# A two-layer diffusion backbone on one core: five raw weight buffers, gate rows kept in DRAM, and the conditioning steps placed anew

## The chip, the core and the metric

The kernel runs on one core of a Trainium2 chip. The metric is the device time of one execution in microseconds (us), lower is better. TensorE (PE in the rows, PEld for its weight loads), VectorE (DVE), ScalarE (ACT), GpSimd (POOL) and SyncE (SP) each work through their own instructions in order; transfers are issued from SP, ACT or POOL.

## The reference

256 latent tokens and 256 context tokens of width 1024 go through two layers. A layer is a half-step gated feed-forward block (1024 to 2 x 2816 to 1024), a token mixer, and a second such block; the mixer of layer 0 is a recurrent RG-LRU block, that of layer 1 a windowed attention. Every block is normed before and after, and modulated by rows that come from a conditioning vector, one for the latent tokens and one for the context tokens:

```python
def modulate(h, g_pre, shift, scale):
    return rms_norm(h, g_pre) * (1 + scale) + shift

def modulation(cond, w, b):                 # w: (1024, 9*1024) for each layer
    m = jax.nn.silu(cond) @ w + b
    return jnp.moveaxis(m.reshape(cond.shape[0], N_MOD, D_MODEL), 1, 0)[:, :, None, :]

def half_ffn_update(h, mod, k, g_pre, g_post, w_in, w_out):
    y = swiglu(modulate(h, g_pre, mod[3 * k], mod[3 * k + 1]), w_in, w_out)
    return h + FFN_RES_WEIGHT * mod[3 * k + 2] * rms_norm(y, g_post)
...
for i in range(DEPTH):                      # x: latent, xc: context
    mx = modulation(c, w_mod[i], b_mod[i]); mc = modulation(c_ctx[None], w_mod[i], b_mod[i])
    x  = half_ffn_update(x, mx, 0, ...);  xc = half_ffn_update(xc, mc, 0, ...)
    ...                                     # mixer, gated by mx[5] and mc[5]
    x  = half_ffn_update(x, mx, 2, ...)     # and xc, except in the last layer
```

Of each layer's nine modulation rows, numbers 2, 5 and 8 are gates (they multiply a block's normed output) and the other six are scales and shifts ahead of a block.

## The kernel before

**Weights.** All weights are fp32 in DRAM. `wslot` (L107) loads 512 KB into a raw buffer `raw` (a ring of three, L47) on SP's queue, casts it on ACT to `whi` (L104) and has DVE form the rest `wlo` (L105); then the raw buffer is free again. `whi` and `wlo` have eight buffers each. `unit` (L120) and `tok_unit` (L135) make each product out of three matmuls (hi x hi, hi x lo, lo x hi), which stand at L127 to L129 and L142 to L144.

**A feed-forward block** (`ffn`, L380) first takes four column blocks j of the inner width, for the 256 latent and then for the 256 context tokens (matmuls of 256 columns), then the other eighteen with all 512 tokens. After each, `glu` (L346) runs: ACT silu into `s2`, DVE product into `a2` (L351), ACT cast into `dh`, DVE rest into `dl`. The 22 blocks are split in three groups; after groups 0 and 1 the product with `w_out` is added up in `y` (eight steps of 21 matmuls), after group 2 `out_last` (L361) finishes tile by tile: `post` (L182) multiplies by the gate row and adds to the residual `x`, `pre` (L196) norms it, `tick` turns the tile (L177, with `diag`) into the `hh` and `hl` of the next block.

**Modulation in the background.** `mod_job` (L289) makes one modulation row and is a generator. `bg(n)`, called after each `glu` (n = 2) and after each step of the `w_out` product (n = 1), advances the current job by n steps. Eight steps load 512 KB of `w_mod` each into a raw buffer and have DVE add it into `m` (L301, once for each of the two conditionings). The ninth sums over the partitions on PE (L307) and then does one of two things. For a scale or shift row: ACT copies the row out of PSUM (L331), PE transposes it into columns (`cols_of`, L256), DVE copies them to `modT`. For a gate row: it is multiplied by a norm row that was loaded into half of a `tmp` buffer (L320), written to DRAM (`spill`, L323) and at once read back, spread over all partitions, into 2 x 512 KB (L327): `grow_m` for the mixers, two `g4` buffers for the feed-forward blocks. These transfers and that of `b_mod` (L296) are issued from ACT's queue. The last gate row (1, 8) is made in `last_ffn` (L882).

**Order.** Tile writes out each engine's order from a model of the times, so a low-priority instruction may stand earlier than its place in the program. Buffers of one tag are handed out in program order.

Of the kernel before, what the change touches and what calls it, by code (L numbers as in the profile page):

```python
# [15 lines left out]
P = 128  # L16
# [20 lines left out]
class Net:  # L37
    def __init__(self, ctx, tc):
# [8 lines left out]
        self.rawp = e(tc.tile_pool(name="rawp", bufs=3))  # L47
# [12 lines left out]
        gm = self.big.tile([P, 2, D], F32, name="grow_m")  # L60
        self.grow_m = [gm[:, 0], gm[:, 1]]
# [29 lines left out]
    def grow_f(self):  # L91
        return [self.g4().rearrange("p a b -> p (a b)") for _ in range(2)]
# [166 lines left out]
    def mods_start(self, w_mod):  # L259
# [15 lines left out]
        row = self.tmp()[:, :512]  # L275
# [13 lines left out]
    def mod_job(self, l, m, conds=(0, 1), grow=None, f=1.0):  # L289
# [3 lines left out]
        for c in conds:  # L293
            acc[c] = self.m4().rearrange("p a b -> p (a b)")
            v.memset(acc[c], 0.0)
            nc.scalar.dma_start(acc[c][0:1], self.b_mod[l : l + 1, m * D : (m + 1) * D])  # L296
# [17 lines left out]
        row = self.tmp()  # L314
        if grow is not None:
            row, gq = row[:, :512], row[:, 512:]
# [63 lines left out]
    def ffn(self, w_in, w_out, bg, after, mid=None):  # L380
# [5 lines left out]
        for s in (LAT, CTX):  # L386
            for j in range(NSPLIT):
# [4 lines left out]
                self.glu(ps[:, 0], ps[:, 1], j, s)  # L392
        for gi, (j0, j1) in enumerate(GROUPS):
# [27 lines left out]
def net_kernel(  # L421
# [117 lines left out]
    def mj(l, m, **kw):  # L539
        return lambda: N.mod_job(l, m, **kw)  # L540

    grow = N.grow_f()
    bg = bg_runner(
        [mj(0, 2, grow=grow, f=0.5), mj(0, 3), mj(0, 4), mj(0, 5, grow=N.grow_m), mj(0, 6), mj(0, 7)]
    )
    N.ffn(ffn_w_in[0, 0], ffn_w_out[0, 0], bg, boundary(grow, 0, 1), load_ctx)

    rg_mixer(N, rg_w_in[0], rg_gate_w[0], rg_w_out[0], rgT, boundary(N.grow_m, 0, 2))

    grow = N.grow_f()  # L550
    bg = bg_runner([mj(0, 8, grow=grow, f=0.5), mj(1, 0), mj(1, 1), mj(1, 3), mj(1, 4)])
    N.ffn(ffn_w_in[0, 1], ffn_w_out[0, 1], bg, boundary(grow, 1, 0))

    grow = N.grow_f()
    bg = bg_runner(
        [mj(1, 2, grow=grow, f=0.5), mj(1, 5, conds=(1,), grow=N.grow_m), mj(1, 6, conds=(1,)), mj(1, 7, conds=(1,))]
    )
    N.ffn(ffn_w_in[1, 0], ffn_w_out[1, 0], bg, boundary(grow, 1, 1))

    attn_mixer(  # L560
        N, attn_w_qkv[0], attn_w_o[0], attn_sink, k_perm, k_rope, k_mask, boundary(N.grow_m, 1, 2, (1,))
    )

    last_ffn(N, ffn_w_in[1, 1], ffn_w_out[1, 1], out)


def rg_mixer(N, w_in, gate_w, w_out, rgT, after):
# [125 lines left out]
    N.out_last(vo, 0, NK, False, TILES, dh, dl, after)  # L693


def attn_mixer(N, w_qkv, w_o, sink, k_perm, k_rope, k_mask, after):
# [89 lines left out]

    wv = [N.wslot([vq[:, 4 * b : 4 * b + 4, NQ + NKVD : NQ + 2 * NKVD]]) for b in range(2)]
# [94 lines left out]
def last_ffn(N, w_in, w_out, out):  # L882
# [3 lines left out]
    grow = N.grow_f()  # L886
    job = N.mod_job(1, 8, conds=(1,), grow=grow, f=0.5)
# [134 lines left out]
```

## Time and profile before

| | us |
|---|---|
| time, median of 3 runs | 1767.45 (1767.33 to 1769.81) |
| span of the profiled execution | 1767.6 |
| PE matmul busy | 1692.1 (96%) |
| DVE busy | 1148.4 (65%) |
| ACT busy | 718.5 (41%) |
| mean DMA rate | 143 GB/s |

The span of the profiled execution, from its first instruction to its last, is within 0.2 us of the median time, so sums over the span are sums over the time. Busy time of PE is what its matmuls occupy, at either of TensorE's clocks; idle time of the other engines costs nothing as long as PE does not wait for them.

### The profile page before, as it was taken

How to read it: one execution, taken by the hardware profiler on the slowest of the kernel's cores; microseconds unless marked ns; L12 is line 12 of the kernel's file. 1: busy time of each engine (PE TensorE's matmuls, PEld its weight loads, DVE VectorE, ACT ScalarE, POOL GpSimd, SP SyncE). 2: the span in 40 equal slices, each digit the busy share in tenths (PEclk: the TensorE clock that was granted, in tenths of full speed). 3: DMA queues.
4: the chain of work that ended last, by engine and by line, in shares of the span. 5: the costliest groups of instructions: out<-in, count | busy, mean ns of one | idle time of the engine just before them, and what ended most of it. 6: DMA issues, size and time to landing. Idle time of an engine off the chain costs nothing.

```text
span 1767.6 us, 22913 instructions
## 1 busy us (share of the span) xinstructions
PE 1692.1 (96%) x8980; PEld 1432.1 (81%) x8980; DVE 1148.4 (65%) x1798; ACT 718.5 (41%) x1148; POOL 0.2 (0%) x4
## 2 busy tenths in 40 slices
PE   5999899999999999989999999998999999999998
PEld 4988688878988798868787898876888888879897
DVE  4756667777878766556874666355333799765554
ACT  3432222235699453122133353132232577564442
POOL 0000000000000000000000000000000000000000
PEclk9999999999999999989999999999999999999999
DMA  8565456572322246445574156576432231057662
GB/s 295 158 177 173 137 155 201 170 222 85 101 75 72 72 139 180 142 132 172 173 210 124 35 145 180 157 225 207 115 96 84 75 104 61 14 153 230 215 207 71
DMA packets 262084, 253.56 MB, mean 143 GB/s; under 512 B 8780, under 2 KB 213028, under 8 KB 261976
## 3 DMA queue, kind: packets, MB, share of 16 engines
q1 hardware_dynamic: 256800, 244.35, 45.7%
q10 hardware_dynamic: 5176, 7.76, 1.5%
q8 instruction: 70, 1.15, 0.3%
q14 instruction: 38, 0.31, 0.1%
HBM read 250.97 MB, written 1.10 MB: 143 GB/s over the span
## 4 chain that ended last, share of the span: by engine, by line
PE 55%; DMA 14%; DVE 13%; ACT 7%; issue 3%; ACTq 0%; DVEq 0%
PE mm L129 11%; PE mm L127 11%; PE mm L128 11%; DMA raw<-in_ffn_w_in_dram 7%; PE mm L142 5%; PE mm L144 5%; PE mm L143 5%; DMA raw<-in_w_mod_dram 4%; DVE wlo L105 4%; DVE m L301 3%; ACT whi L104 3%; DMA raw<-in_ffn_w_out_dram 2%; PE st L838 1%; PE st L177 1%; ACT tmp L217 1%
## 5 line engine op out<-in xcount | busy, mean ns | idle before, releaser
L127 PE MATMUL mm<-hh,whi 128*128 128x512 f32 (+1 forms) x1808 | 617.1, 341 | 2.5 <-ACT hh L247 2.1
L129 PE MATMUL mm<-hh,wlo 128*128 128x512 f32 (+1 forms) x1808 | 616.4, 341 | 2.0 <-DVE wlo L105 2.0
L128 PE MATMUL mm<-hl,whi 128*128 128x512 f32 (+1 forms) x1808 | 615.9, 341 | 0.1
L104 ACT CAST whi<-raw 128x1024 fp32r<-128x1024 f32 x322 | 332.1, 1035 | 569.5 <-DMA raw<-in_ffn_w_in_dram 252.3
L105 DVE TENSOR_TENSOR wlo<-raw,whi 128x1024 fp32r<-128x1024 f32 x322 | 386.1, 1203 | 270.3 <-ACT whi L104 267.8
L127 PEld LDWEIGHTS mm<-hh,whi 128*128 128x128 f32 x1808 | 346.1, 192 | 47.5 <-issue 4.2
L129 PEld LDWEIGHTS mm<-hh,wlo 128*128 128x128 f32 x1808 | 346.2, 192 | 39.5 <-DVE wlo L105 2.6
L128 PEld LDWEIGHTS mm<-hl,whi 128*128 128x128 f32 x1808 | 345.8, 191 | 38.0 <-DVE hl L249 0.7
L301 DVE SCALAR_TENSOR_TENSOR m<-raw,cs,m 128x1024 f32<-128x1024 f32 x224 | 279.6, 1278 | 50.2 <-DMA raw<-in_w_mod_dram 49.2
L142 PE MATMUL mm<-whi,dh 128*128 128x512 f32 x592 | 232.8, 396 | 7.5 <-ACT dh L104 5.0
L143 PE MATMUL mm<-wlo,dh 128*128 128x512 f32 x592 | 232.5, 393 | 1.1 <-DVE wlo L105 0.9
L144 PE MATMUL mm<-whi,dl 128*128 128x512 f32 x592 | 231.9, 392 | 0.5 <-DVE dl L105 0.5
L142 PEld LDWEIGHTS mm<-whi,dh 128*128 128x128 f32 x592 | 112.1, 190 | 38.2 <-ACT dh L104 5.5
L143 PEld LDWEIGHTS mm<-wlo,dh 128*128 128x128 f32 x592 | 112.2, 189 | 26.0 <-DVE wlo L105 3.4
L144 PEld LDWEIGHTS mm<-whi,dl 128*128 128x128 f32 x592 | 112.0, 189 | 24.3 <-DVE dl L105 1.2
L351 DVE TENSOR_TENSOR a<-s,mm 128x512 f32<-128x512 f32 (+1 forms) x96 | 54.3, 566 | 77.9 <-PE mm L129 59.9
L104 ACT CAST dh<-a 128x512 fp32r<-128x512 f32 (+1 forms) x96 | 50.5, 527 | 132.1 <-DVE a L351 132.0
L350 ACT ACTIVATE s<-mm 128x512 f32<-128x512 f32 (+1 forms) x96 | 48.2, 502 | 72.8 <-PE mm L129 70.0
L105 DVE TENSOR_TENSOR dl<-a,dh 128x512 fp32r<-128x512 f32 (+1 forms) x96 | 54.5, 567 | 14.4 <-ACT dh L104 14.1
L177 PE MATMUL st<-diag,xres 128*128 128x128 f32 x352 | 47.8, 292 | 13.1 <-DVE diag L170 10.3
L177 PEld LDWEIGHTS st<-diag,xres 128*128 128x128 f32 x352 | 45.1, 204 | 17.8 <-DVE diag L170 10.1
L217 ACT ACTIVATE tmp<-st,modT,A 128x128 f32<-128x128 f32 x144 | 55.2, 470 | 6.4 <-PE st L177 6.3
(189 smaller groups left out, 1364.5 us busy)
## 6 DMA issues: line engine op xcount, KB each, us to landing
raw<-in_ffn_w_in_dram SPq DMA_DIRECT2D x176, 512.0 KB
raw<-in_w_mod_dram SPq DMA_DIRECT2D x128, 512.0 KB
raw<-in_ffn_w_out_dram SPq DMA_DIRECT2D x82, 512.0 KB
wm<-in_w_mod_dram SPq DMA_DIRECT2D x16, 512.0 KB
raw<-in_rg_w_in_dram SPq DMA_DIRECT2D x16, 512.0 KB
raw<-in_attn_w_qkv_dram SPq DMA_DIRECT2D x12, 512.0 KB
raw<-in_rg_gate_w_dram SPq DMA_DIRECT2D x16, 256.0 KB
raw<-in_rg_w_out_dram SPq DMA_DIRECT2D x8, 512.0 KB
```

Source lines behind the costliest of these rows:

```text
L104: self.nc.scalar.copy(hi, src)
L105: self.nc.vector.tensor_tensor(lo, src, hi.bitcast(F32), op=ALU.subtract)
L127: nc.tensor.matmul(out, a, xh, start=(k == 0), stop=False)
L128: nc.tensor.matmul(out, a, xl, start=False, stop=False)
L129: nc.tensor.matmul(out, b, xh, start=False, stop=(k == nk - 1))
L142: nc.tensor.matmul(out, a, wh, start=(k == 0), stop=False)
L143: nc.tensor.matmul(out, a, wl, start=False, stop=False)
L144: nc.tensor.matmul(out, b, wh, start=False, stop=(k == nk - 1))
L177: self.nc.tensor.matmul(ps[:, q * P : (q + 1) * P], self.x[:, t, k * P : (k + 1) * P], dg, start=True, stop=True)
L217: nc.scalar.activation(hf[:, k * P : (k + 1) * P], ps[:, q * P : (q + 1) * P], AF.Identity, bias=S[:, k, cond : cond + 1], scale=A[:, k, c ...
L301: v.scalar_tensor_tensor(acc[c], raw, self.cs[:, k, c : c + 1], acc[c], op0=ALU.mult, op1=ALU.add)
L351: nc.vector.tensor_tensor(b, a, pu, op=ALU.mult)
```

## The change

Five things are changed together.

1. The ring `raw` gets five buffers in place of three; `grow_m` (8 KB of each partition) is gone.
2. A gate row stays in DRAM (`spill`, kept in `rows`) after it is made. `load_rows` spreads it over the partitions where it is wanted: just ahead of `out_last` in a feed-forward block and in `rg_mixer` (into two `g4` buffers), after the keys in `attn_mixer` (into the context's residual tile 0, which the second layer's end does not need), and at the start of `last_ffn` (residual tile 1).
3. All these small transfers, and those of `b_mod` and the norm row, go to GpSimd's queue. The copied rows and norm rows stand in `s2` and `a2` instead of `tmp`.
4. For a scale or shift row there is a `yield` between ACT's copy and PE's transposes, so they are two steps (ten a job).
5. In the first part of each `ffn` there is one step more after each `glu` (in the very first block only for the context half), and the job of row (1, 8) moves from `last_ffn` to the block before the attention.

```diff
-        self.rawp = e(tc.tile_pool(name="rawp", bufs=3))
+        self.rawp = e(tc.tile_pool(name="rawp", bufs=5))
...
-        gm = self.big.tile([P, 2, D], F32, name="grow_m")
-        self.grow_m = [gm[:, 0], gm[:, 1]]
+        self.rows = {}
...
+    def grow_g4(self):
+        return {c: self.g4().rearrange("p a b -> p (a b)") for c in range(2)}
+
+    def load_rows(self, key, grow):
+        for c, dst in grow.items():
+            for hb in range(2):
+                j = 2 * hb + c
+                self.nc.gpsimd.dma_start(
+                    dst[:, hb * 512 : hb * 512 + 512], self.rows[key][j : j + 1].to_broadcast((P, 512))
+                )
+        return grow
...
-            nc.scalar.dma_start(acc[c][0:1], self.b_mod[l : l + 1, m * D : (m + 1) * D])
+            nc.gpsimd.dma_start(acc[c][0:1], self.b_mod[l : l + 1, m * D : (m + 1) * D])
...
+        if f is not None:
+            gq = self.s2()
...
-                nc.scalar.dma_start(gq[32 * j : 32 * j + 32], self.norm_g[l, gi : gi + 1, cc].to_broadcast((32, 512)))
+                nc.gpsimd.dma_start(gq[32 * j : 32 * j + 32], self.norm_g[l, gi : gi + 1, cc].to_broadcast((32, 512)))
+            row = self.a2()
             v.scalar_tensor_tensor(row, ps, f * RS, gq, op0=ALU.mult, op1=ALU.mult)
...
-            nc.scalar.dma_start(spill, row[0:P:32])
-            for c in conds:
-                for hb in range(2):
-                    j = 2 * hb + c
-                    nc.scalar.dma_start(grow[c][:, hb * 512 : hb * 512 + 512], spill[j : j + 1].to_broadcast((P, 512)))
+            nc.gpsimd.dma_start(spill, row[0:P:32])
+            self.rows[l, m] = spill
             yield
             return
-        row = row[:, :512]
+        row = self.s2()
         nc.scalar.copy(row, ps)
+        yield
         tv = self.cols_of(row)
...
                 self.glu(ps[:, 0], ps[:, 1], j, s)
+                if mid is None or s is CTX:
+                    bg(1)
...
                 bg(1000)
+                rows()
                 self.out_last(vo, j0, j1, True, TILES, self.dh, self.dl, after)
...
+    lat = dict(conds=(1,))
+    ffn(0, 0, [mj(0, 2, f=0.5), mj(0, 3), mj(0, 4), mj(0, 5, f=1.0), mj(0, 6), mj(0, 7)], 0, 1, load_ctx)
+    rg_mixer(N, rg_w_in[0], rg_gate_w[0], rg_w_out[0], rgT, lambda grow: boundary(grow, 0, 2))
+    ffn(0, 1, [mj(0, 8, f=0.5), mj(1, 0), mj(1, 1), mj(1, 3), mj(1, 4)], 1, 0)
+    ffn(
+        1,
+        0,
+        [mj(1, 2, f=0.5), mj(1, 5, f=1.0, **lat), mj(1, 6, **lat), mj(1, 7, **lat), mj(1, 8, f=0.5, **lat)],
+        1,
+        1,
     )
...
+        lambda: after_attn.update(N.load_rows((1, 5), {1: N.x[:, 0]})),
+        boundary(after_attn, 1, 2, (1,)),
     )
...
+    last_ffn(N, ffn_w_in[1, 1], ffn_w_out[1, 1], N.load_rows((1, 8), {1: N.x[:, 1]}), out)
...
+    grow = N.load_rows((0, 5), N.grow_g4())
+    N.out_last(vo, 0, NK, False, TILES, dh, dl, after(grow))
...
-    grow = N.grow_f()
-    job = N.mod_job(1, 8, conds=(1,), grow=grow, f=0.5)
...
-        if j >= 6:
-            next(job, None)
```

## Rows read from the trace of the kernel before

**Rows 1.** The page's first lines: span, and busy time and share of each engine.

```profile
span 1767.6 us, 22913 instructions
PE 1692.1 (96%) x8980; PEld 1432.1 (81%) x8980; DVE 1148.4 (65%) x1798; ACT 718.5 (41%) x1148; POOL 0.2 (0%) x4
```

**Rows 2.** What PE waited for, over the span: us in total, times, longest us.

```profile
PE st L256 <- ACT tmp L331: 16.8, 4, 6.6
PE st L177 <- DVE diag L170: 10.3, 8, 1.9
...
PE mm L142 <- ACT dh L104: 5.0, 1, 5.0
PE st L898 <- DVE dl L105: 3.1, 3, 1.8
...
PE mm L129 <- DVE wlo L105: 2.0, 2, 1.2
```

**Rows 3.** Stretches of the span: from:to, length, then busy us (and instructions) of PE, PEld, DVE, ACT and POOL, the granted TensorE clock (1.00 is full), the DMA engines' busy share, GB/s.

```profile
186.80:192.40 5.60, 0.00 (x0) 0.00 (x0) 2.80 (x4) 2.15 (x3) 0.00 (x0) 0.69 0.19 40
192.40:195.80 3.40, 3.35 (x10) 2.86 (x11) 2.51 (x5) 0.00 (x0) 0.00 (x0) 0.50 0.34 134
777.10:782.80 5.70, 5.56 (x15) 4.55 (x16) 4.78 (x8) 0.09 (x1) 0.00 (x0) 0.50 0.20 80
936.70:939.90 3.20, 3.20 (x10) 2.72 (x11) 2.52 (x6) 0.00 (x0) 0.00 (x0) 0.50 0.77 247
1230.80:1236.80 6.00, 5.40 (x12) 3.81 (x13) 2.94 (x6) 0.02 (x1) 0.00 (x0) 0.50 0.95 282
1639.60:1643.00 3.40, 3.40 (x12) 2.72 (x11) 1.38 (x2) 0.73 (x2) 0.00 (x0) 0.50 0.83 240
```

**Rows 4.** The instructions around the first of these stalls, in order of time on PE, ACT and SP: start, duration, and in brackets the idle time before and what ended it.

```profile
192.45 1.11 PE L256 MATMUL st<-ident,tmp 128*128 128x128 f32 x4 [5.68 <-ACT tmp L331]
...
188.36 1.04 ACT L104 CAST whi<-raw 128x1024 fp32r<-128x1024 f32 x1 [5.06 <-DMA raw<-in_ffn_w_in_dram]
191.82 0.58 ACT L331 COPY tmp<-st 128x512 f32<-128x512 f32 x1
...
184.09 0.38 SPq L113 DMA_DIRECT2D raw<-in_ffn_w_in_dram  x1
```

**Rows 5.** What SP's queue waited for before it could issue a load, over the span (L113 weights, L299 `w_mod`).

```profile
SPq L113 <- DVE wlo L105: 770.9, 201, 63.8
SPq L299 <- DVE m L301: 187.9, 50, 17.6
```

**Rows 6.** What ACT waited for, over the span.

```profile
ACT whi L104 <- DMA raw<-in_ffn_w_in_dram: 252.3, 105, 8.3
ACT whi L104 <- DMA raw<-in_ffn_w_out_dram: 133.8, 57, 16.2
```

**Rows 7.** Stretches as in rows 3: the first part of the second block, the start, a feed-forward block, the last block, and the end of the block before the attention.

```profile
617.00:640.00 23.00, 21.08 (x156) 19.91 (x155) 19.07 (x43) 18.68 (x40) 0.00 (x0) 1.00 0.64 181
20.00:40.00 20.00, 16.39 (x100) 9.03 (x99) 8.23 (x28) 7.46 (x12) 0.00 (x0) 0.88 0.97 331
740.00:760.00 20.00, 20.00 (x90) 16.56 (x89) 14.27 (x12) 5.66 (x8) 0.00 (x0) 1.00 0.80 232
1600.00:1700.00 100.00, 96.52 (x656) 88.08 (x655) 58.04 (x63) 41.10 (x54) 0.00 (x0) 0.98 0.72 221
1240.00:1360.00 120.00, 120.00 (x536) 98.47 (x535) 44.55 (x51) 34.46 (x41) 0.00 (x0) 1.00 0.35 102
```

**Rows 8.** DVE and PE at the end of a group in the block before the attention, in order of time.

```profile
1223.31 1.29 DVE L301 SCALAR_TENSOR_TENSOR m<-raw,cs,m 128x1024 f32<-128x1024 f32 x1 [2.95 <-DMA raw<-in_w_mod_dram]
...
1228.29 1.28 DVE L301 SCALAR_TENSOR_TENSOR m<-raw,cs,m 128x1024 f32<-128x1024 f32 x1 [2.56 <-DMA raw<-in_w_mod_dram]
1229.49 0.68 DVE L351 TENSOR_TENSOR a<-s,mm 128x512 f32<-128x512 f32 x1
...
1230.87 0.80 PE L142 MATMUL mm<-whi,dh 128*128 128x512 f32 x1 [5.03 <-ACT dh L104]
```

**Rows 9.** DVE in `last_ffn` around one of PE's waits for `dl`, in order of time.

```profile
1637.00 1.28 DVE L301 SCALAR_TENSOR_TENSOR m<-raw,cs,m 128x1024 f32<-128x1024 f32 x1 [1.37 <-DMA raw<-in_w_mod_dram]
1638.20 0.42 DVE L105 TENSOR_TENSOR dl<-a,dh 128x256 fp32r<-128x256 f32 x1
```

**Rows 10.** DVE and PE in the first part of the block before the attention, in order of time: the end of the last tile's norm (L170) and the turn that needs it (L177).

```profile
1032.27 1.28 DVE L301 SCALAR_TENSOR_TENSOR m<-raw,cs,m 128x1024 f32<-128x1024 f32 x1 [0.67 <-DMA raw<-in_w_mod_dram]
...
1034.28 1.28 DVE L301 SCALAR_TENSOR_TENSOR m<-raw,cs,m 128x1024 f32<-128x1024 f32 x1
1035.47 0.28 DVE L170 TENSOR_SCALAR diag<-ident,small 128x128 f32<-128x128 f32 x1
...
1035.81 1.38 PE L177 MATMUL st<-diag,xres 128*128 128x128 f32 x10 [1.89 <-DVE diag L170]
```

**Rows 11.** ACT's small transfers at the end of the first gate row's job, in order of time.

```profile
140.42 0.58 ACTq L323 DMA_DIRECT2D spill<-tmp  x1
143.67 1.80 ACTq L327 DMA_DIRECT2D g<-spill  x4
```

**Rows 12.** DVE at the end of `rg_mixer`: the last reading of a `g4` buffer and the first use of the gate row.

```profile
577.94 0.68 DVE L678 TENSOR_TENSOR y<-g,g 128x512 f32<-128x512 f32 x1
...
594.67 1.41 DVE L190 SCALAR_TENSOR_TENSOR tmp<-mm,small,grow_m 128x512 f32<-128x512 f32 x2
```

More of the change, by code (lines that the diff above doesn't have):

```diff
@@ L89, in a2 @@
         return self.ph.tile([P, T], dt, tag="a2", name=self.nm("a2"), bufs=2)
-    def grow_f(self):
-        return [self.g4().rearrange("p a b -> p (a b)") for _ in range(2)]
+    def grow_g4(self):
[8 more added lines that the diff above has]
+        return grow
     def c(self, shape, dt, name):
@@ L274, in mods_start @@
                     )
-        row = self.tmp()[:, :512]
+        row = self.s2()
         nc.scalar.copy(row, ps)
@@ L287, in mods_start, with mod_job @@
                     )
-    def mod_job(self, l, m, conds=(0, 1), grow=None, f=1.0):
+    def mod_job(self, l, m, conds=(0, 1), f=None):
         nc = self.nc
@@ L313, in mod_job @@
                 )
-        row = self.tmp()
-        if grow is not None:
-            row, gq = row[:, :512], row[:, 512:]
+        if f is not None:
+            gq = self.s2()
             gi = 3 + m // 3
@@ L319, in mod_job @@
                 cc = slice((j // 2) * 512, (j // 2) * 512 + 512)
-                nc.scalar.dma_start(gq[32 * j : 32 * j + 32], self.norm_g[l, gi : gi + 1, cc].to_broadcast((32, 512)))
+                nc.gpsimd.dma_start(gq[32 * j : 32 * j + 32], self.norm_g[l, gi : gi + 1, cc].to_broadcast((32, 512)))
+            row = self.a2()
             v.scalar_tensor_tensor(row, ps, f * RS, gq, op0=ALU.mult, op1=ALU.mult)
             spill = self.tc.dram_tile([4, 512], F32, name=self.nm("spill"))
-            nc.scalar.dma_start(spill, row[0:P:32])
-            for c in conds:
-                for hb in range(2):
-                    j = 2 * hb + c
-                    nc.scalar.dma_start(grow[c][:, hb * 512 : hb * 512 + 512], spill[j : j + 1].to_broadcast((P, 512)))
+            nc.gpsimd.dma_start(spill, row[0:P:32])
+            self.rows[l, m] = spill
             yield
             return
-        row = row[:, :512]
+        row = self.s2()
         nc.scalar.copy(row, ps)
+        yield
         tv = self.cols_of(row)
@@ L378, in out_last, with ffn @@
                 self.tick(2)
-    def ffn(self, w_in, w_out, bg, after, mid=None):
+    def ffn(self, w_in, w_out, bg, rows, after, mid=None):
         nc = self.nc
@@ L540, in mj, with ffn @@
         return lambda: N.mod_job(l, m, **kw)
-    grow = N.grow_f()
-    bg = bg_runner(
-        [mj(0, 2, grow=grow, f=0.5), mj(0, 3), mj(0, 4), mj(0, 5, grow=N.grow_m), mj(0, 6), mj(0, 7)]
-    )
[L546 to L556, printed above, removed]
-    )
[L558 to L564, printed above, removed]
+    def ffn(l, k, jobs, l2, k2, mid=None):
+        grow = {}
+        N.ffn(
+            ffn_w_in[l, k],
+            ffn_w_out[l, k],
+            bg_runner(jobs),
+            lambda: grow.update(N.load_rows((l, 2 + 6 * k), N.grow_g4())),
+            boundary(grow, l2, k2),
+            mid,
+        )
+    lat = dict(conds=(1,))
[8 more added lines that the diff above has]
+        1,
+    )
+    after_attn = {}
+    attn_mixer(
+        N,
+        attn_w_qkv[0],
+        attn_w_o[0],
+        attn_sink,
+        k_perm,
+        k_rope,
+        k_mask,
+        lambda: after_attn.update(N.load_rows((1, 5), {1: N.x[:, 0]})),
+        boundary(after_attn, 1, 2, (1,)),
+    )
+    last_ffn(N, ffn_w_in[1, 1], ffn_w_out[1, 1], N.load_rows((1, 8), {1: N.x[:, 1]}), out)
 def rg_mixer(N, w_in, gate_w, w_out, rgT, after):
@@ L691, in rg_mixer, with attn_mixer @@
         prev = ins
-    N.out_last(vo, 0, NK, False, TILES, dh, dl, after)
-def attn_mixer(N, w_qkv, w_o, sink, k_perm, k_rope, k_mask, after):
+    grow = N.load_rows((0, 5), N.grow_g4())
+    N.out_last(vo, 0, NK, False, TILES, dh, dl, after(grow))
+def attn_mixer(N, w_qkv, w_o, sink, k_perm, k_rope, k_mask, rows, after):
     nc = N.nc
@@ L785, in attn_mixer @@
                 )
+    rows()
     wv = [N.wslot([vq[:, 4 * b : 4 * b + 4, NQ + NKVD : NQ + 2 * NKVD]]) for b in range(2)]
@@ L879, in attn_mixer, with last_ffn @@
     proj(1, 1)
-def last_ffn(N, w_in, w_out, out):
+def last_ffn(N, w_in, w_out, grow, out):
     nc = N.nc
@@ L885, in last_ffn @@
     vo = w_out.rearrange("(j p) c -> p j c", p=P)
-    grow = N.grow_f()
-    job = N.mod_job(1, 8, conds=(1,), grow=grow, f=0.5)
     po = {}
```

## The prediction, made before the changed kernel was run

> **What bounds the kernel now.** I read the page first: PE is busy in 1692.1 of 1767.6 us, DVE in 65% and ACT in 41% [rows 1]. The matmuls themselves stay as they are, so no edit can gain more than PE's idle 75.5 us and the time it works at the half clock. The next view is what PE waited for [rows 2]: the largest wait, 16.8 us in four pieces, is that of the transposes (L256) for ACT's copy; then come 10.3 us for the norm's `diag`, 5.0 for one `dh`, 3.1 for `dl`, 2.0 for `wlo`. The third view, short stretches around these waits, shows the second price [rows 3]: PE sits idle from 186.8 to 192.4, and then runs at clock 0.50 (1.2 instead of 2.4 GHz) until 195.8. Each longer idle time is followed by such a stretch, and half of a stretch is lost.
>
> Why is a copy of 0.58 us late by 5.7? The instructions around it show it [rows 4]: ACT's queue is in order, and ahead of the copy stood a cast that waited 5.06 us for its weights. That load was issued at 184.09, only when one of the three raw buffers came free. SP's queue tells the same over the span: 770.9 us, 201 times, it waited for a raw buffer that `wlo` still held, and 187.9 us for one held by `m` [rows 5]. ACT in turn waited 252.3 and 133.8 us for loads [rows 6]. PE is mostly covered, since eight `whi` and `wlo` stand ahead of it; what reaches it is what is queued on ACT or DVE behind a late load: a copy, a `dh`, a `dl`, a `diag`.
>
> **The change part by part.**
>
> *Transposes a step later.* The four waits cost 16.8 us, and the half-clock stretches after three of them 3.40, 5.70 and 3.20 us, of which half is lost: 1.7 + 2.85 + 1.6 = 6.15. Together 22.95 us. I went through the calls of `bg` to see what stands between the two steps now. Seven of ten jobs get 21 to 48 matmuls between copy and transposes (at 20.00 / 90 = 0.222 us each [rows 7], 4.7 us or more): `dh`, copy and all are done by then. In three, both steps fall into one call, with nothing between: (0, 6) after block 17, (0, 7) at the end of the first feed-forward block, and (1, 6) after block 9. For those the old risk stays: 3 of 10 jobs at a mean of 22.95 / 3 = 7.65 us for each stall, and 3 of 10 stalled at length before, is 3 x 0.3 x 7.65 = 6.9 us; with a deeper ring I take half, 3.4 (bounds 0 and 22.95). Gain **19.6**.
>
> *Five raw buffers.* Is the ring or the DMA rate the limit? With sixteen loads in flight at the start the chip moved 331 GB/s at a DMA share of 0.97; in a feed-forward block with three it reached 232 at 0.80, and it needs some 196 there (four loads of 0.524 MB for each 48 matmuls of 0.222 us = 10.7 us) [rows 7]. So three buffers leave little above the need, and five leave up to 331. Where does a late load reach PE other than by the copies? At the end of a group [rows 8] DVE's product `a` stands behind two `m`, which waited 2.95 and 2.56 us for `w_mod`; PE waited 5.03 us for the `dh` made from it and then ran six us at the half clock, 3.0 lost: 8.0 us. I take four fifths, 6.4 (bounds 0 and 8.0; the same `m` can stand there with its load in place). Of the waits for `wlo`, 2.0 us [rows 2], I take 1.5. Gain **7.9**.
>
> *The job of row (1, 8).* It leaves the last block, which ran at 221 GB/s and kept PE idle for 3.5 of 100 us [rows 7], and whose `dl` stood behind an `m` that waited 1.37 us for its load [rows 9]. The waits for `dl`, 3.1 us, and half of the 3.40 at half clock go: **4.8**. In the block before the attention it costs eight `m` of 1.28 = 10.2 us of DVE, and there DVE is busy 44.6 of 120 us at 102 GB/s: nothing, while that room lasts. Its sums on PE (L307) are made in the one place as in the other.
>
> *Steps in the first part.* The first `w_mod` steps of the two later blocks are now due while the last tile is still normed and turned. What that does is seen in the block before the attention [rows 10]: two `m` got in between the norm's small operations, 1.28 us each and 0.67 of waiting, and PE waited 1.89 us for `diag`. In the block before that, none did. I charge two more `m` in each, 2 x 2 x 1.28 = 5.1 us: **-5.0**. Bounds: 0, if `diag` keeps its priority, and four steps of 2.56 us in each of the three first parts, 30.7.
>
> *Small transfers on GpSimd's queue, rows in DRAM.* ACT loses its issues (one spill 0.58, four row loads 1.80, [rows 11]); PE didn't wait for those, so I take 0. The bounds: a gain of nothing, since ACT is idle 59% of the span; a loss where a row comes late. `post` needs the row first about 11 us after `out_last` starts, and in the feed-forward blocks the buffers and the spilled rows are ready long before. In `rg_mixer` the `g4` buffers come free only at 577.94 + 0.68 = 578.6, and the row is used at 594.67 [rows 12]: 16 us. From a spill's issue to the row load that needs it it is 143.67 - 141.00 = 2.7 us [rows 11]; four loads of 256 KB at 232 GB/s take 4.5 more, 7.2 in all: covered. POOL did 0.2 us of work before [rows 1]; nothing else is queued there but the next blocks' `b_mod`, which came after that point before, too. The swap of `tmp` for `s2` and `a2` costs nothing while `glu`, every 10.7 us, holds its buffer for 1 to 2 us: one of two is always free.
>
> One rule speaks against this edit. The Trainium skill (SBUF — State Buffer, SBUF: two separate sides) says that a transfer issued from GpSimd needs descriptors which GpSimd cannot write while VectorE runs an operation that takes both of its ports, and gives 3.1 us in place of 0.62 for such a transfer. No run here shows such a transfer yet. By its figure four row loads take an estimated 12.4 us, still under the 16; its case is the last rival below.
>
> **Sum.** 19.6 + 7.9 + 4.8 - 5.0 = 27.3 us; 1767.6 - 27.3 = 1740.3, say **1740**. The span and the median of the runs, 1767.45, are the same for this purpose.
>
> **The rivals.**
> - *The rate, not the ring, is the limit.* Five loads share what three shared, each lands later, and ACT and DVE wait as long as before. For it: the share of 0.95 at 282 GB/s in one stretch [rows 3]. Against it: SP's waits [rows 5], and 232 against 331 [rows 7]. Then the ring gives none of its 7.9 and the three unparted jobs cost 6.9: 27.3 - 7.9 - 3.5 = 15.9, **1752**.
> - *The ring does more.* The loads land so early that `diag`, `dh` and the unparted copies meet no queue: the remaining 3.4 and 1.6 are gained, nothing is charged for the first parts, and half of the 10.3 for `diag` goes: 27.3 + 3.4 + 1.6 + 5.0 + 5.1 = 42.4, **1725**.
> - *The turn is not later.* The order is written from modelled times, and the transposes at 192.45 [rows 4] did not stand straight behind their sums; if the planner puts them back to the copy, 19.6 is lost: 7.7 remain, **1760**. Against it: their place in the program is now behind a block's matmuls, which are ready.
> - *Slower: DVE is overrun in the first parts.* In 617 to 640 DVE was busy 19.07 of 23 us [rows 7], and four steps more of 2.56 are 10.2: 29.3 in 23. If `hl` and `diag` stand behind them, PE waits 6.3 us in each of three first parts, and a wait of that length brought 1.6 to 3 us at the half clock: some 9 each, 27 in place of the 5 charged: 1767.6 - 27.3 + 22 = 1762. From 32.3 / 3 = 10.8 us each the kernel is slower; with loads waited for in between, 13 each gives **1774**. Against it: PE turns the last tile only 14 us into the block, and `pre` has priority.
> - *Slower: the row comes late in `rg_mixer`.* Beyond 16 us every us is one of PE's, and the half clock follows. It decides when the load ends 27 us late, 43 us for four loads: 11 each, four times what the 2.7 us [rows 11] bear out; at 13 each the time is 1767.6 - 27.3 + 36 = **1776**.
>
> **How the numbers follow.** Chances: the forecast (1733 to 1747) 0.42; the rate 0.20; the ring does more 0.16; the turn not later 0.06; gains and new waits cancel 0.05; DVE overrun 0.08, and the row late 0.03. Runs of one kernel lie 0.14% apart, so 0.2% (3.5 us) is what can be told from no change. Faster: 0.42 + 0.20 + 0.16 + 0.06 = 0.84, less 0.01 for the upper edge of the DVE case, which I count as slower; same 0.05; slower 0.12. The range runs from the far side of "the ring does more" (bounds of the same terms, 5 us further: 1720) to the third rival's 1760, and leaves out the 0.05 and 0.12, and some 0.03 at either edge.
>
> **What the new profile would show.** Right: no wait of L256 for the copy over 1 us except at the three unparted jobs; SP's waits for `wlo` and ACT's for loads well under 770.9 and 386; rates above 232 GB/s inside a block; no wait for `dl` in the last block. Wrong: a wait for `diag` above 1.9 us early in the second or third block, clock 0.50 in a first part, PE waiting for `post` after `rg_mixer`, or ACT's waits for loads as long as before.

## The result and the profile after

The changed kernel takes 1725.24 us (median; 1724.68 to 1725.57) where the kernel before took 1767.39 beside it: a ratio of 0.9766 [0.9752, 0.9780], 42.2 us faster. The forecast was 1740 with a range of 1720 to 1760. The direction and the range hold, the size doesn't: the gain is half as large again as the 27.3 us of the sum, and the time lands on the rival "the ring does more", 1725.

The head of the page after, the lines that answer to [rows 1]:

```profile
span 1723.8 us, 23005 instructions
PE 1678.0 (97%) x8980; PEld 1425.6 (83%) x8980; DVE 1139.6 (66%) x1798; ACT 716.5 (42%) x1148; POOL 40.3 (2%) x82
```

The span is 43.8 us shorter, and the two numbers of PE divide it. Its idle time goes from 75.5 to 1723.8 - 1678.0 = 45.8 us, 29.7 less; its busy time goes from 1692.1 to 1678.0 with the same 8980 instructions, 14.1 less. The mean granted clock rises from 0.985 to 0.993, and busy time times clock is the same before and after (1692.1 x 0.985 = 1666.7, 1678.0 x 0.993 = 1666.3), so the 14.1 us are time at the half clock that is gone. In every run that gives both, the span is 1.7 to 2.3 us below the time of its own execution, so that the span of before lies as near as 0.2 us to the median time is chance, and the spans differ by 1.6 us more than the median times do.

What PE waited for after the change (us in total, times, longest), the lines that answer to [rows 2]:

```profile
PE st L185 <- DVE diag L178: 6.2, 4, 2.5
...
PE mm L150 <- ACT dh L112: 2.4, 1, 2.4
...
PE mm L137 <- DVE wlo L113: 1.0, 2, 0.7
PE st L264 <- ACT s L336: 0.8, 1, 0.8
```

The transposes (L264, before L256) wait 0.8 us in place of 16.8, `diag` 6.2 in place of 10.3, one `dh` 2.4 in place of 5.0, `wlo` 1.0 in place of 2.0. Of the 3.1 us for `dl` in the last block nothing is left. These five are 16.0 + 4.1 + 2.6 + 1.0 + 3.1 = 26.8 of the 29.7 us.

What ACT waited for before it could cast a weight, the answer to [rows 6]. First one line of the kernel before that was not shown, then three of after:

```profile
ACT whi L104 <- PE mm L128: 112.1, 49, 3.9
```

```profile
ACT whi L112 <- PE mm L136: 244.8, 97, 5.1
ACT whi L112 <- DMA raw<-in_ffn_w_in_dram: 134.5, 59, 10.2
...
ACT whi L112 <- DMA raw<-in_ffn_w_out_dram: 64.0, 32, 7.3
```

The change shows in these lines. ACT's waits for a load fall from 252.3 + 133.8 to 134.5 + 64.0 us, and its waits for PE to give a `whi` slot back rise from 112.1 to 244.8. The weights now stand ready in front of PE more often: while a cast waits for a slot, PE still has the weights in the other slots to work on, and PE's own waits show none for a `whi`.

SP's queue, the answer to [rows 5], shows little of that:

```profile
SPq L121 <- DVE wlo L113: 752.0, 194, 63.9
...
SPq L307 <- DVE m L309: 87.6, 40, 7.2
```

It waited 752.0 us for a buffer that `wlo` held, before 770.9. The wait at the `w_mod` loads for one that `m` held fell from 187.9 to 87.6, but the same wait at the weight loads (L121, before L113) rose from 129.3 to 246.6. A ring that is kept full waits for its oldest buffer, here with five as with three.

### The profile page after: what moved, and what is told of

The parts are those of the page before. It is cut to its first block, busy times and chain, and to the rows that moved or that the text cites. A ratio compares the mean times of both kernels' runs of the same rounds, so it can differ in the third digit from the quotient of the medians.

```text
span 1723.8 us, 23005 instructions
## 1 busy us (share of the span) xinstructions
PE 1678.0 (97%) x8980; PEld 1425.6 (83%) x8980; DVE 1139.6 (66%) x1798; ACT 716.5 (42%) x1148; POOL 40.3 (2%) x82
## 4 chain that ended last, share of the span: by engine, by line
PE 78%; DVE 9%; ACT 6%; DMA 4%; issue 3%; ACTq 0%; DVEq 0%
PE mm L136 15%; PE mm L135 15%; PE mm L137 15%; PE mm L150 7%; PE mm L152 7%; PE mm L151 7%; DVE m L309 2%; DMA raw<-in_ffn_w_in_dram 2%; DVE wlo L113 2%; PE st L861 2%; PE st L185 1%; ACT tmp L225 1%; ACT whi L112 1%; DMA raw<-in_ffn_w_out_dram 1%; PE st L315 1%
## 5 line engine op out<-in xcount | busy, mean ns | idle before, releaser
L112 ACT CAST whi<-raw 128x1024 fp32r<-128x1024 f32 x322 | 331.4, 1038 | 517.5 <-PE mm L136 244.8
L113 DVE TENSOR_TENSOR wlo<-raw,whi 128x1024 fp32r<-128x1024 f32 x322 | 382.6, 1202 | 204.9 <-ACT whi L112 202.2
L113 DVE TENSOR_TENSOR dl<-a,dh 128x512 fp32r<-128x512 f32 (+1 forms) x96 | 54.4, 567 | 18.9 <-ACT dh L112 18.6
```

The costliest lines, as they stand in the source:

```text
L112: self.nc.scalar.copy(hi, src)
L113: self.nc.vector.tensor_tensor(lo, src, hi.bitcast(F32), op=ALU.subtract)
```

## The experiments

Each is the kernel before, the changed one, or the kernel of "The ring alone", with the edits that are named. Times are medians, and each ratio is to the kernel before on the same chip. The experiments ran on three chips: the turn alone, the change with three buffers, without the turn and with ACT's queue on the first (kernel before 1771.35 us); the ring alone with five and three buffers, no steps and the last job on the second (1771.18); four buffers, the split ring, the parted jobs and six buffers on the third (1771.55). The changed kernel was timed apart from all of them, beside 1767.39. Where two from different groups are compared, the difference of their ratios is given too. None leaves work out.

**The turn alone.** The kernel before, with only the new step between the copy and the transposes:

```diff
         row = row[:, :512]
         nc.scalar.copy(row, ps)
+        yield
         tv = self.cols_of(row)
```

> The kernel before with the yield between copy and transposes alone; nothing else changed. The prediction's sum: the turn takes 16 to 20 us by itself (22.95 less what the jobs still keep unparted, at the old ring's full risk), so about 1749. Rival 'the ring does more': with three raw buffers the copies that share a call still stall, and the turn alone brings under 12 us. Rival 'the turn is not later': under 3 us.

Measured: 1757.78 us (1757.16 to 1758.38), 0.9929 [0.9910, 0.9948], some 12.5 us faster (13.6 by medians). The transposes' wait in this kernel:

```profile
PE st L256 <- ACT tmp L331: 7.9, 2, 7.6
```

So half of the 16.8 us went, where the sum booked 19.6 of 22.95 us for the turn. The rival "the turn is not later" falls, and the term is too large for a ring of three.

**The change with three raw buffers.**

```diff
-        self.rawp = e(tc.tile_pool(name="rawp", bufs=5))
+        self.rawp = e(tc.tile_pool(name="rawp", bufs=3))
```

> The changed kernel with three raw buffers; all else as changed. The prediction's sum: it loses the ring's 7.9 and 3.5 for unparted copies, 11 us, about 1737. Rival 'the ring does more': it loses 20 us or more, 1745 or above, with PE waits for dl, wlo and diag back. Rival 'the rate is the limit': within 3 us of 1725.

Measured: 1765.16 us (1759.66 to 1766.83), 0.9959 [0.9944, 0.9975]. Everything but the ring, together, brings about 7 us, less than the turn alone brought on the same chip: 1765.16 against 1757.78, in ranges that don't meet. So with three buffers the other edits (rows in DRAM, GpSimd's queue, the steps in the first parts, the last job's move) cost some 7 us together, where the sum had them at 4.8 - 5.0, next to nothing. Here the three jobs that the prediction called unparted can be seen at work. The transposes' wait over the span, and its three pieces in order of time (start, duration, in brackets the idle time and what ended it):

```profile
PE st L264 <- ACT s L336: 18.0, 3, 8.4
```

```profile
335.57 0.69 PE L264 MATMUL st<-ident,s 128*128 128x128 f32 x2 [5.94 <-ACT s L336]
385.99 0.86 PE L264 MATMUL st<-ident,s 128*128 128x128 f32 x4 [3.62 <-ACT s L336]
1184.77 1.11 PE L264 MATMUL st<-ident,s 128*128 128x128 f32 x4 [8.43 <-ACT s L336]
```

These are the jobs (0, 6), (0, 7) and (1, 6), the three named from the code; the other seven never wait. But all three of three stall, not 3 of 10 as before, and they wait as long as the four did before the change. What stands ahead of the third on ACT is what [rows 4] showed, in this kernel and, for the same copy, in the changed one:

```profile
1180.20 1.04 ACT L112 CAST whi<-raw 128x1024 fp32r<-128x1024 f32 x1 [2.52 <-DMA raw<-in_ffn_w_in_dram]
...
1183.19 1.04 ACT L112 CAST whi<-raw 128x1024 fp32r<-128x1024 f32 x1 [1.44 <-DMA raw<-in_ffn_w_in_dram]
1184.14 0.58 ACT L336 COPY s<-st 128x512 f32<-128x512 f32 x1
```

```profile
1151.48 1.05 ACT L112 CAST whi<-raw 128x1024 fp32r<-128x1024 f32 x1 [0.42 <-PE mm L136]
...
1153.02 0.58 ACT L336 COPY s<-st 128x512 f32<-128x512 f32 x1
```

With three buffers the two casts ahead of the copy wait for loads, 2.52 and 1.44 us; with five the cast ahead waits 0.42 us, and for PE.

**The change without the turn, and with ACT's queue.** Two kernels, each the changed one with one part undone:

```diff
         nc.scalar.copy(row, ps)
-        yield
         tv = self.cols_of(row)
```

> The changed kernel without the yield: copy and transposes are one step again, ring of five. The prediction's sum: without the turn the four copies can stall again but at half the risk under the deeper ring, so it loses 8 to 20 us, 1733 to 1745, with waits of L256's successor for the copy in the rows. Rival 'the ring does more': the five buffers alone keep the copies on time, loss under 4 us.

```diff
-                self.nc.gpsimd.dma_start(
+                self.nc.scalar.dma_start(
...
-            nc.gpsimd.dma_start(acc[c][0:1], self.b_mod[l : l + 1, m * D : (m + 1) * D])
+            nc.scalar.dma_start(acc[c][0:1], self.b_mod[l : l + 1, m * D : (m + 1) * D])
...
-            nc.gpsimd.dma_start(spill, row[0:P:32])
+            nc.scalar.dma_start(spill, row[0:P:32])
```

> The changed kernel with its small transfers on ACT's queue instead of GpSimd's; all else as changed. The prediction's sum puts this edit at nothing: 1725 +- 3. Rival: the 15 us that the sum lacks came from ACT, whose queue no longer holds casts behind a spill or a row that waits; then it loses 8 us or more. Rival 'rows come late on GpSimd': it gains.

Measured: without the turn 1731.22 us (1730.61 to 1732.61), 0.9780 [0.9761, 0.9799]; with the small transfers on ACT's queue 1728.99 (1726.61 to 1730.04), 0.9762 [0.9738, 0.9785]. The changed kernel ran beside a kernel before of 1767.39, so there are two readings: against its 1725.24 the turn is worth 6.0 us once the ring is there, against its ratio of 0.9766 only 0.0014 x 1767 = 2.5. Either is well under the 12.5 that it brought alone. The queue gives 3.8 us by medians and nothing by ratios: whether it brings anything stays open, and neither reading shows a cost of it.

**The ring alone.** The kernel before has no room for five buffers beside `grow_m`. So the rows stay in DRAM in both of these kernels, and all other parts are undone: ACT's queue, no turn, no step in the first parts, the job of row (1, 8) back in `last_ffn`. The first has five raw buffers, the second three.

```diff
-        self.rawp = e(tc.tile_pool(name="rawp", bufs=5))
+        self.rawp = e(tc.tile_pool(name="rawp", bufs=3))
```

> Rows in DRAM (that frees the room) and five raw buffers, with all else as before: small transfers on ACT's queue, copy and transposes one step, no steps added in the first parts, the job of row (1, 8) in last_ffn. Theory A, the ring by itself carries most: it gains 25 us or more over the kernel before, 1742 or less. Theory B, the ring pays only with the steps moved: it gains the 11.4 of the prediction's sum, 1756 or so. Compare with the same kernel with three buffers (e6).

> Rows in DRAM with three raw buffers, all else as before (see e5). Both theories: within 4 us of the kernel before. If it is slower by more, the new places of the rows (s2 and a2, a load before each out_last) cost something that the five buffers hide.

Measured: five 1728.27 us (1727.18 to 1729.75), 0.9766 [0.9751, 0.9782]; three 1774.66 (1769.71 to 1779.46), 1.0024 [1.0006, 1.0041]. Rows in DRAM, with the swap of `tmp` for `s2` and `a2`, are by themselves a little slower than the kernel before; two more buffers on top of them are worth 46.4 us, more than the whole change. The pages' heads and two of PE's waits, first of five, then of three:

```profile
PE 1677.0 (97%) x8980; PEld 1426.1 (83%) x8980; DVE 1140.8 (66%) x1798; ACT 716.1 (42%) x1148; POOL 0.2 (0%) x4
...
PE st L264 <- ACT s L336: 7.2, 3, 2.8
```

```profile
PE 1694.0 (95%) x8980; PEld 1434.0 (81%) x8980; DVE 1148.0 (65%) x1798; ACT 718.8 (40%) x1148; POOL 0.2 (0%) x4
...
PE st L264 <- ACT s L336: 16.8, 4, 5.9
...
PE mm L150 <- ACT dh L112: 5.1, 1, 5.1
```

With three, all is as in [rows 2]: four waits of the transposes, 16.8 us together, and one `dh` of 5.1. With five, and with copy and transposes still in one step, the transposes wait 7.2 us, in pieces of at most 2.8, and PE's busy time is 17.0 us less, the half clock (busy time times clock is 1666.9 in both). One thing these two don't part: Tile writes each engine's order from modelled times, and with five buffers many casts on ACT, and much on DVE, stand at other places in the order than with three. The 46.4 us are those of the deeper ring together with the order that is written for it.

**Four buffers.** The kernel of the ring alone, with four buffers.

```diff
-        self.rawp = e(tc.tile_pool(name="rawp", bufs=5))
+        self.rawp = e(tc.tile_pool(name="rawp", bufs=4))
```

> The kernel of e5 (rows in DRAM, all else as before) with four raw buffers. Three gave 1774.7 and five 1728.3. If a little headroom over the need is enough, four bring most of it: 1738 or less, 36 of the 46 us. If what counts is how many loads are under way while two buffers are held by w_mod, each buffer brings its part: 1745 to 1758.

Measured: 1739.14 us (1734.79 to 1740.61), 0.9810 [0.9792, 0.9829]. The dose is 1774.7, 1739.1, 1728.3 us for three, four and five: the first buffer brings 35.5, the second 10.9. Four ran on another chip; by ratios it is 0.0214 x 1771 = 38 and 0.0044 x 1771 = 8. What half clock goes, goes with the first: PE is busy 1694.0, 1677.8 and 1677.0 us, so the second buffer takes back idle time alone.

**A ring for the weights, another for `w_mod`.** Is it the number of buffers, or that `w_mod` takes them from the weights? The kernel of the ring alone with three buffers for weights and two of its own for `w_mod`, five in all (its lines stand one further down):

```diff
-        self.rawp = e(tc.tile_pool(name="rawp", bufs=5))
+        self.rawp = e(tc.tile_pool(name="rawp", bufs=3))
+        self.rawm = e(tc.tile_pool(name="rawm", bufs=2))
...
-            raw = self.raw()
+            raw = self.rawm.tile([P, D], F32, tag="rawm", name=self.nm("rawm"))
```

> The kernel of e5 with the same five buffers in two rings: three for the weights, two for w_mod. If the number of loads under way is all that counts, 1728 +- 4. If the shared ring made it (weights fill all five when no w_mod is due), it lies well above, 1740 or more; if w_mod in the shared ring held up weights, it is faster than 1724.

Measured: 1742.92 us (1741.23 to 1745.26), 0.9837 [0.9821, 0.9852]: 14.7 us slower than the shared five, 31.7 faster than the shared three, both on another chip; by ratios 12.6 and 33. The intervals don't meet. PE's new waits say where, and the instructions around them why. The waits, then ACT in the attention:

```profile
PE mm L151 <- DVE tmp L199: 5.3, 2, 4.3
PE st L761 <- ACT s L113: 4.2, 4, 3.4
```

```profile
1389.45 1.04 ACT L113 CAST whi<-raw 128x1024 fp32r<-128x1024 f32 x1 [4.42 <-DMA raw<-in_attn_w_qkv_dram]
1390.40 0.36 ACT L113 CAST s<-mm 128x256 fp32r<-128x256 f32 x1
```

First, in the attention no job runs, so the two buffers of `w_mod` stand empty and three are left: a cast waits 4.42 us for its load, the small cast of `s` stands behind it, and PE waits 3.4 us for that. The other place is the end of `rg_mixer`, on DVE:

```profile
601.82 1.28 DVE L310 SCALAR_TENSOR_TENSOR m<-rawm,cs,m 128x1024 f32<-128x1024 f32 x1
...
603.09 1.28 DVE L310 SCALAR_TENSOR_TENSOR m<-rawm,cs,m 128x1024 f32<-128x1024 f32 x1
604.28 1.41 DVE L199 SCALAR_TENSOR_TENSOR tmp<-mm,small,g 128x512 f32<-128x512 f32 x2
```

The steps `m` of `w_mod` stand between the norm's small operations and ahead of `post` (L199), for which PE waits 4.3 us; I read it as `w_mod` being loaded early by a ring of its own. That would be the mechanism of the rival "DVE is overrun", one stage earlier than I had put it. ACT's wait for `ffn_w_in` is the least of these kernels here:

```profile
ACT whi L113 <- DMA raw<-in_ffn_w_in_dram: 93.2, 47, 5.7
```

yet the kernel is slower than the shared five. Its casts also wait longest for PE's slots, 372.2 us. So neither sum of waits, off the bounding engine, orders the kernels.

**No steps in the first parts.**

```diff
                 self.glu(ps[:, 0], ps[:, 1], j, s)
-                if mid is None or s is CTX:
-                    bg(1)
```

> The changed kernel without the added steps in the first parts. The prediction's sum charged 5.0 us for them: without them 1720. Rival: the steps are worth their place, because they take loads out of the crowded middle of a block: without them 1728 or more.

Measured: 1724.73 us (1723.96 to 1725.14), 0.9745 [0.9731, 0.9760], against 1725.24 and 0.9766 with them. By medians the steps cost 0.5 us, and so do the two profiled spans (1723.8 and 1723.3); by ratios it is 0.0021 x 1767 = 3.7, with intervals that overlap. Either is under the 5.0 of the sum, and not parted from nothing. On this same chip the ring alone took 1728.27, in a range that doesn't meet this one: beside five buffers, the turn, the queue and the last job bring 3.5 us all together.

**The last job back in the last block.**

```diff
-        [mj(1, 2, f=0.5), mj(1, 5, f=1.0, **lat), mj(1, 6, **lat), mj(1, 7, **lat), mj(1, 8, f=0.5, **lat)],
+        [mj(1, 2, f=0.5), mj(1, 5, f=1.0, **lat), mj(1, 6, **lat), mj(1, 7, **lat)],
...
+    job = N.mod_job(1, 8, conds=(1,), f=0.5)
...
+        if j >= 6:
+            next(job, None)
+            if j == 14:
+                N.load_rows((1, 8), grow)
```

> The changed kernel with the job of row (1, 8) back in last_ffn, one step after each block from j = 6, its row loaded after j = 14. The prediction's sum: 4.8 us slower, 1730, with waits for dl in the last block back. If the five buffers alone take those waits away: 1725 +- 2, and no wait for dl above 1 us.

Measured: 1727.10 us (1725.60 to 1727.41), 0.9756 [0.9739, 0.9774]. Against the changed kernel's 1725.24 and 0.9766 the move is worth 1.9 us of the 4.8 by medians, by ratios nothing. PE has no wait for `dl` in the last block here either, so the ring has taken what the move was booked for.

**The three unparted jobs parted.** The kernel without steps in the first parts, in which the copy now ends its call of `bg`, except in the last call of a block, which runs all jobs to their end:

```diff
-        yield
+        yield True
...
-                    next(state["g"])
-                    n -= 1
+                    n = 0 if next(state["g"]) and n < 100 else n - 1
```

> The changed kernel without the added steps in the first parts, and with the copy always ending its call, so that all ten jobs have matmuls between copy and transposes. e7, without the parting, gave 1724.7 with 2.0 us of waits for the copy. If those waits are what the yield is for: 1722 to 1724 and no such wait but at a block's end. If the time hangs on other waits: 1725 +- 2.

Measured: 1722.23 us (1721.19 to 1723.10), 0.9719 [0.9704, 0.9733], 2.5 us under the kernel it is made from, whose range it doesn't meet, though that ran on another chip; by ratios it is 0.0026 x 1771 = 4.6, with intervals that just overlap. The transposes' wait is 0.2 us, where it was 2.0.

**Six buffers.** The same base, with six; the room comes from the mask and the rounded identity of the attention, which move into parts of `hh` and `hl` that are free there, and from smaller constants and statistics tiles (`soft`, sixteen buffers to twelve), so this is not the ring by itself.

```diff
-        self.rawp = e(tc.tile_pool(name="rawp", bufs=5))
+        self.rawp = e(tc.tile_pool(name="rawp", bufs=6))
...
-    N.ones = N.c([P, P], F32, "ones")
+    N.ones = N.c([P, 32], F32, "ones")
...
-    identr = N.c([P, P], F32R, "identr")
+    identr = N.hl[:, 0, 0:P]
```

> The kernel of e7 with six raw buffers; for room the mask and one unit matrix of the attention stand in the context half of hh and hl once the values are made, and the sums' ones are 32 columns. If five buffers are still short: 1719 or less, with ACT's waits for loads below the 171 of e7. If the ring is no longer the limit: 1725 +- 3, or slower by the later mask.

Measured: 1722.52 us (1720.50 to 1723.80), 0.9719 [0.9702, 0.9737]. A sixth buffer, with what makes room for it, is worth about as much as parting the jobs: 2.2 us by medians, 4.6 by ratios, with intervals that overlap. Both kernels are faster than the changed one, with intervals that don't meet its own. The two together were not run.

## Why the prediction was right in direction and short in size

**The step that failed** is *Five raw buffers*, 7.9 us. I priced a deeper ring by the one wait that I could trace to it beside the transposes, the `dh` of [rows 8], with bounds of 0 and 8.0, and booked the rest to the edits that touch the other waits' lines. But [rows 4] had already said that the copy was late because a load was: the transposes' wait, the `dl` behind an `m` that waited for its load [rows 9] and the `dh` are one cause seen at three lines. The ring alone gained 46.4 us. The upper bound of 8.0 was the mistake: it should have been everything behind a late load. By the working's own rows that is 22.95 for the transposes, 8.0 for `dh`, 4.8 for `dl` and 2.0 for `wlo`, 37.75 us with their half clock. Even this falls short of 46.4; where the rest comes from was not traced.

**The terms don't add.** The turn brought 12.5 us with three buffers; with five, the turn, the queue and the job's move together brought 3.5 on one chip, where the sum had 24.4 for them. Turn and ring cure the same stalls, the turn by putting work between the copy and PE, the ring by letting the copy come on time. A sum in which each stall is booked once, to one edit, gave the total fairly, but its terms are no forecast of the edits. That the time lies in the range is in part luck: the turn was booked too high and the ring too low. So is the hit of the rival "the ring does more": its mechanism is by and large the one that the runs bear out, but its 1725 still books the whole wait for the copy to the turn.

**Where the missing us are**, by the working's own pieces. The times are 14.9 us short of the sum, the spans, from which the pieces are read, 43.8 - 27.3 = 16.5. The sum's 27.3 us split into idle time of 17.9 (14.3 of the transposes' 16.8, 4.0 for `dh`, 1.5 for `wlo`, 3.1 for `dl`, less 5.0 for the first parts) and 9.4 at the half clock. Measured are 29.7 and 14.1. Of the 11.8 us of idle time 5.0 are the charge for the first parts, which is not to be seen in the balance, 4.1 the waits for `diag`, which shrank instead of growing, 1.7 the transposes; 1.0 is left over of small waits. The remaining 4.7 us of half clock are found by subtraction alone: they would stand behind waits to which I had given no such price.

**The rate was not the limit.** The rival at 1752 falls on the ring alone, where two more buffers gained 46.4 us. The landing times fit that. The loads with three buffers (the changed kernel but for its ring) and with five (the changed kernel); the last column is the median time from issue to landing:

```profile
raw<-in_ffn_w_in_dram SPq DMA_DIRECT2D x176, 512.0 KB, 4.7
raw<-in_w_mod_dram SPq DMA_DIRECT2D x128, 512.0 KB, 4.1
raw<-in_ffn_w_out_dram SPq DMA_DIRECT2D x82, 512.0 KB, 3.9
```

```profile
raw<-in_ffn_w_in_dram SPq DMA_DIRECT2D x176, 512.0 KB, 4.5
raw<-in_w_mod_dram SPq DMA_DIRECT2D x128, 512.0 KB, 4.2
raw<-in_ffn_w_out_dram SPq DMA_DIRECT2D x82, 512.0 KB, 4.5
```

The loads of `ffn_w_in` and `w_mod` land as soon as before, those of `ffn_w_out` 0.6 us later. That holds for five buffers only: the sixteen loads of `wm` at the start, which need no ring, take 7.5 us in the changed kernel. (Before the change they were issued over 15.23 us from 4.87 on, so the first of them should have landed ahead of the stretch with 331 GB/s in [rows 7], for which the prediction counts all sixteen in flight.) Stretches of the changed kernel (columns as in [rows 3]): one in the second feed-forward block, then the last block, as [rows 7]:

```profile
740.00:760.00 20.00, 20.00 (x90) 16.54 (x89) 13.85 (x14) 9.58 (x12) 0.00 (x0) 1.00 0.87 261
```

```profile
1590.00:1690.00 100.00, 100.00 (x706) 94.12 (x705) 52.20 (x60) 43.82 (x60) 0.00 (x0) 1.00 0.57 176
```

261 GB/s where the three buffers gave 232. The two stretches hold other work, but of the six stretches of 20 us from 700 to 820 the highest is 221, 227 and 232 GB/s in kernels with three buffers (the change with three, the rows alone, before) and 261 and 286 with five (the change, the ring alone): there was room above 232, and a deeper ring used it. In the last block PE has no idle time at all, where it had 3.5 of 100 us, and the clock is full.

**The first parts.** [rows 10] was misread. In the kernel before, PE waited as long for `diag` at the start of the second block, where no `m` stood between the norm's operations:

```profile
637.10 2.05 PE L177 MATMUL st<-diag,xres 128*128 128x128 f32 x16 [1.92 <-DVE diag L170]
```

So the 1.89 us of [rows 10] need not be the work of the two `m`. In the changed kernel neither block has such a wait for `diag`. What the added steps do delay is `hl`, and with it the matmuls behind the turn. DVE and then PE, early in the third block:

```profile
1010.58 1.28 DVE L309 SCALAR_TENSOR_TENSOR m<-raw,cs,m 128x1024 f32<-128x1024 f32 x1
1011.78 0.28 DVE L178 TENSOR_SCALAR diag<-ident,small 128x128 f32<-128x128 f32 x1
...
1013.50 2.48 DVE L309 SCALAR_TENSOR_TENSOR m<-raw,cs,m 128x1024 f32<-128x1024 f32 x2
1015.89 0.69 DVE L113 TENSOR_TENSOR hl<-tmp,hh 128x512 fp32r<-128x512 f32 x1
```

```profile
1015.72 0.74 PE L135 MATMUL mm<-hh,whi 128*128 128x256 f32 x4 [1.56 <-ACT hh L112]
```

```profile
1015.70:1019.20 3.50, 3.30 (x19) 3.10 (x20) 3.50 (x6) 1.84 (x5) 0.00 (x0) 0.75 0.63 199
```

The `m` stand ahead of `diag` and of `hl`, PE waits 1.56 us for `hh`, and the granted clock is 0.75 over the next 3.5 us. The very first block has a wait of that kind too, behind four `m`, which the kernels without the steps don't have:

```profile
PE mm L136 <- DVE hl L257: 1.5, 1, 1.5
```

These two waits and a quarter of the 3.5 us are an estimated 3.9 us, not far under the charge. But the kernel without the steps has waits that this one lacks (2.6 us at the sums, L315, and 3.1 more for `diag`), so that all the steps together cost 0.5 us by medians and spans, 3.7 by ratios. The mechanism, `m` ahead of PE's next operand on DVE, is there; the line that I took it from was not an instance that can be told from the norm's own time, and the charge left out what the steps relieve elsewhere.

**The rows in DRAM and GpSimd's queue** were priced at nothing, and no run shows a cost of the queue. The four row loads at the end of `rg_mixer` (POOL) and the first use of the row (DVE):

```profile
567.32 2.15 POOL L97 DMA_DIRECT2D g<-spill  x4 [237.65 <-DVE y L699]
```

```profile
576.99 1.41 DVE L198 SCALAR_TENSOR_TENSOR tmp<-mm,small,g 128x512 f32<-128x512 f32 x2
```

They are issued in 2.15 us, against 1.80 on ACT [rows 11], and land in 4.1 us by the median, so by that the last is there at 567.32 + 2.15 + 4.1 = 573.6, three us before the first use. The cover was 9.7 us from the issue, not the 16 that [rows 12] let me expect, since the time from the buffer's last reading to the use is shorter here. The Trainium skill (SBUF — State Buffer, SBUF: two separate sides) would have a transfer issued from GpSimd take 3.1 us in place of 0.62 while VectorE runs an operation that takes both of its ports. By its figure an estimate of four such transfers in a row is 12.4 us, and the last would have been late here. The trace shows no such delay: 2.15 us for the four issues, and nobody waited for a row. It doesn't test the figure, though: DVE ran TENSOR_TENSOR in nearly all of those 2.15 us, and no run shows which of its operations take both ports.

**What the text said the new profile would show.** No wait of L264 over 1 us outside the three jobs: right, and none in them either. Rates above 232 GB/s and no wait for `dl` in the last block: right. ACT's waits for loads well under 386: right, 198.5. SP's waits for `wlo` well under 770.9: wrong, and wrongly chosen, since a full ring waited here at every depth. Clock at half in a first part: it fell there, to 0.75 over 3.5 us. A wait for `diag` above 1.9 us early in the second or third block: none; the longest, 2.52 us, stands at the end of the attention. PE waiting for `post` after `rg_mixer`: none.

**What stays open.** Whether the 3.8 us of GpSimd's queue are there at all; and why the rows in DRAM with three buffers are 0.24% slower than the kernel before; and how much of the ring's gain is the buffers themselves and how much the order that Tile writes for them.

## What to carry to other kernels

If one late load shows up at several lines, behind an in-order queue, price its cure once and at the cause: the bound of a deeper ring is every wait behind a late load, with the half clock after each, and not the one wait that no other edit touches. Look for what the engines in front of the bounding one wait for: here the casts' waits moved from loads to the consumer's slots as the ring grew, while the queue that issues the loads waited about as long with three buffers as with five. Take that as a sign that a ring was too shallow, not as a ranking: the split ring moved the most, and was slower than the shared five. Before a ring is split by kind of load, look at the stages in which one kind is absent.

## What the runs showed of the hardware

Five loads in place of three that may be under way left the median time to landing of 512 KB about as it was: 4.5 against 4.7 us for `ffn_w_in`, 4.2 against 4.1 for `w_mod`, 4.5 against 3.9 for `ffn_w_out`. The granted clock after an idle time, in the kernel with three buffers, over the 3.5 us that follow the first and the 3.4 that follow the third of its stalls (5.94 and 8.43 us), and in the changed kernel over the 5.4 us that follow the wait of 0.81 us for the copy:

```profile
335.50:339.00 3.50, 3.43 (x11) 2.95 (x12) 3.17 (x7) 0.64 (x2) 0.49 (x1) 0.57 0.42 130
...
1184.70:1188.10 3.40, 3.33 (x10) 2.84 (x11) 2.23 (x2) 0.02 (x1) 0.00 (x0) 0.50 0.46 161
```

```profile
326.60:332.00 5.40, 5.35 (x26) 4.51 (x27) 4.90 (x7) 0.26 (x1) 0.97 (x2) 1.00 0.19 70
```

The short wait costs its own 0.81 us and nothing else, the long ones half of the stretch behind them as well. A value between 0.50 and 1.00 is a stretch spent partly at 1.2 and partly at 2.4 GHz. In between there is no clean order by length. The kernel of the ring alone has three such stalls, of 2.36, 2.06 and 2.82 us, and these are the stretches behind them:

```profile
187.00:190.40 3.40, 3.35 (x13) 2.80 (x14) 2.76 (x6) 0.00 (x0) 0.00 (x0) 0.72 0.53 155
377.40:381.00 3.60, 3.56 (x18) 3.03 (x19) 3.48 (x8) 1.89 (x2) 0.00 (x0) 1.00 1.16 307
762.60:766.00 3.40, 3.32 (x10) 2.84 (x11) 2.79 (x6) 0.02 (x1) 0.00 (x0) 0.50 0.53 153
```

The stall of 2.06 us left the clock full, and the one of 2.82 was followed by half clock like the long ones; the 1.56 us of the third block's first part were followed by 0.75. So a ring that only shortens the stalls, as this one does, can take back half-clock time as well as idle time, but not after each of them. The 17.0 us of PE's busy time between its two runs are the sum over all stalls that went or shrank, and were not split among them.
